# Undilated key-major scores with the queries in natural order, and an exponential that reads its PSUM columns by residue of four

## The chip, the cores and the metric

The kernel runs on one core of one Trainium2 chip. The metric is the device time of one execution in microseconds (us). Five engines work beside each other on their own instruction queues: TensorE (PE in the profile, its weight loads as PEld), VectorE (DVE), ScalarE (ACT), GpSimd (POOL) and SyncE (SP), which issues nearly all DMAs. Matrix products land in PSUM, everything else lives in SBUF or in DRAM.

## The reference, cut to what matters

One decoder layer is computed for a prompt of 2048 tokens and a group of 32 sample tokens: a normalised input projection, retention heads and attention heads beside each other, an output projection, a SwiGLU block and a final norm. The change lies in the attention of the prompt: 8 heads of 64 dimensions, each with three patterns of window and dilation, (128, 1), (512, 4) and (2048, 16).

```
def banded_window_attention(q, k, v, n_back):
    ...
    s = jnp.einsum('nbihd,nbjhd->nbhij', qb, kb, preferred_element_type=jnp.float32) * ATT_SCALE
    ...
    mask = (dist >= 0) & (dist <= n_back) & (kj[:, None, :] >= 0)
    s = jnp.where(mask[None, :, None], s, -jnp.inf)
    lse = jax.nn.logsumexp(s, axis=-1)
    p = jnp.exp(s - lse[..., None])
    o = jnp.einsum('nbhij,nbjhd->nbihd', p, vb.astype(jnp.float32))

def dilated_attention_prompt(q, k, v):
    for window, dil in DILATED_GROUPS:
        ...
    return combine_by_denominator(outs, lses)
```

In every pattern a query sees the 129 keys at distances 0, dil, 2 dil, ... The three outputs are added with the weights of their softmax denominators, which is one softmax with a common maximum and a common sum.

## The kernel before

The program runs in phases: an input phase (`phase_in`), `attention`, `mixing`, the output projection (`phase_out`) and the SwiGLU block (`phase_ff`). Next to each other in time they share the engines, and the instruction order on each engine is the order in which the Python code emits them.

`attention` works head by head, and inside a head over 20 groups of units. A unit is 128 keys and the queries that see them. Groups 0 to 3 have dilation 16 (four units of 128 queries each). Then come, four times, two groups of dilation 4 and two groups of dilation 1, each of two units of 256 queries; where a unit stands at the end of the sequence it has 128. So a head has 8 groups of dilation 1, and the last of them has 384 query columns in place of 512.

For each group three things are done on TensorE:

- `weights` (tile `aB`, key-major: keys on partitions, queries in columns). One product of an identity with a mask (L863, or L865 where the two units differ in width) fills the PSUM bank with 0 or -1e30. Each unit then adds two products to its columns: L878 (128 rows: the keys' high and low halves against the high half of the queries) and L879 (66 rows: the low half of the queries, and the negated maximum). ScalarE takes the exponential out of PSUM (`p`, L883) and rounds it (`ph`, L884), and GpSimd, in some groups VectorE, forms the remainder (`pl`, L885). The bank pool of `aB` has two buffers.
- `values` (tile `acc`, L928 to L930), three products for each 128 query columns, with `ph` and `pl` as the moving operand. It comes three groups later (`LAG = 3`).
- `row_max` of a later head (tile `aS`, L811 and L813, query-major), whose maxima VectorE takes (L817). It runs in 16 of a head's 20 groups, and not at all beside the last head.

In the values of a dilation-1 group the query columns have to stand by residue of four (`e r i` in the code: 128-blocks, residue, index), because one accumulator bank of 512 columns (`acc`, `o_` in `values`) serves both dilation 4 and dilation 1 and is laid out by residue. Before the change this order is made by the score products: for `step == 1` the moving operand, the queries in SBUF, is read with a step of four fp32 elements, and the mask has a second copy in the same order:

```
mk = maskr[:, 1 if groups[gi][0][0] == 1 else 0]
...
if step == 1:
    s = s.rearrange("p (e r i) -> p e r i", r=4, i=32)
    q1, q2 = (a[:, t0:t0 + n].rearrange("p (e i r) -> p e r i", r=4, i=32) for a in (q1, q2))
```

The two mask copies are written once, by two casts each on ScalarE (L1003, L1004); for the second copy L1003 reads SBUF with the same step of four. In dilation-4 and dilation-16 groups the queries are read with a step of 4 and 16 elements, since they are the tokens of one residue.

Of the kernel before, what the change touches and what calls it, by code (L numbers as in the profile page):

```python
# [8 lines left out]
F32R = mybir.dt.float32r  # L9
AF = mybir.ActivationFunctionType  # L10
# [90 lines left out]
def hybrid_step(ctx: ExitStack, tc: tile.TileContext, i: dict, o: dict):  # L101
    nc = tc.nc
    pe, act, dve, pool, sp = nc.tensor, nc.scalar, nc.vector, nc.gpsimd, nc.sync

    def f32(ap):
        return ap.bitcast(F32)
# [639 lines left out]
    def attention(after):  # L746
# [4 lines left out]
        ro = P("ao", 1)  # L751
# [1 line left out]
        jk = P("aj", 2)  # L753
        pS = P("apS", 3, PSUM)
        mask = ro.tile([128, 256], F32, name="mask")
        maskr = ro.tile([128, 2, 384], F32R, name="maskr")
        names = ("kst", "qhh", "qll", "k2")
        sets = [[ro.tile([128, T], F32R, name=f"{n}0") for n in names]]
        H = {}
# [1 line left out]
        def load_qk(h):  # L761
            d = H[h] = {}
            ks, qh, ql, k2 = sets[h % 3]
            r = slice(h * 64, h * 64 + 64)
            for a in range(2):
                dma(ks[64 * a:64 * a + 64], d_qk[1][a][r, :])
                dma(qh[64 * a:64 * a + 64], d_qk[0][0][r, :])
            dma(ql[0:64], d_qk[0][1][r, :])
            if h > 2:
                dma(ql[64:66], d_z)  # L770
            dma(k2[0:64], d_qk[1][0][r, :])
            d.update(ks=ks, qh=qh, ql=ql, k2=k2, m=mp.tile([128, 48], F32, tag="m", name="m"))
# [11 lines left out]
        def unit(dil, b, r=0):  # L784
            if dil == 16:
                return 16, r, False, False, r, 32 + r
            if dil == 1:
                return 1, 128 * b, b > 0, b < 15, b, b
            return 4, 512 * b + r, b > 0, b < 3, 4 * b + r, 16 + 4 * b + r

        groups = [[unit(16, 0, 4 * g + r) for r in range(4)] for g in range(4)]
# [63 lines left out]
        def weights(h, gi):  # L855
            d = H[h]
            ps = pB.tile([128, 512], F32, tag="b", name="aB")
            off = 0
            ns = [256 if u[3] else 128 for u in groups[gi]]
            mk = maskr[:, 1 if groups[gi][0][0] == 1 else 0]  # L860
            if len(set(ns)) == 1:
                m_ = mk[:, 0:ns[0]].rearrange("p (o n) -> p o n", o=1).to_broadcast([128, len(ns), ns[0]])
                pe.matmul(ps[:, 0:sum(ns)].rearrange("p (o n) -> p o n", o=len(ns)), identr, m_, start=True, stop=False)  # L863
            else:
                pe.matmul(ps[:, 0:384], identr, mk, start=True, stop=False)  # L865
            for x, (step, t0, _, nxt, kt, _) in enumerate(groups[gi]):
                n = ns[x]
                s = ps[:, off:off + n]
                off += n
                kc = slice(t0, t0 + 127 * step + 1, step)  # L870
                q1, q2 = d["qh"], d["ql"][0:66]
                if step == 1:

                    s = s.rearrange("p (e r i) -> p e r i", r=4, i=32)
                    q1, q2 = (a[:, t0:t0 + n].rearrange("p (e i r) -> p e r i", r=4, i=32) for a in (q1, q2))
                else:
                    q1, q2 = (a[:, t0:t0 + (n - 1) * step + 1:step] for a in (q1, q2))
                pe.matmul(s, d["ks"][:, kc], q1, start=False, stop=False)  # L878
                pe.matmul(s, d["k2"][0:66, kc], q2, start=False, stop=(x == len(ns) - 1))  # L879
            p = pp.tile([128, 512], F32, tag="p", name="p")  # L880
            hi = ptp.tile([128, 512], F32R, tag="ph", name="ph")
            lo = ptp.tile([128, 512], F32R, tag="pl", name="pl")
            act.activation(p[:, 0:off], ps[:, 0:off], AF.Exp)  # L883
            act.copy(hi[:, 0:off], p[:, 0:off])  # L884
            (dve if gi in DV[h] else pool).tensor_tensor(lo[:, 0:off], p[:, 0:off], f32(hi[:, 0:off]), ALU.subtract)  # L885
            return h, gi, hi, lo
# [94 lines left out]
        def ones(t):  # L981

            for x, v in ((3, 1.0), (2, 0.0)):
                dve.tensor_scalar(t[x][64:66], zero[64:66, 0:1].to_broadcast([2, T]), v, None, ALU.add)
# [12 lines left out]
        junk = jk.tile([128, 512], F32, tag="j", name="junk")[:, 0:256]  # L997
        dma(junk, i["k_maskt"])
        load_qk(0)
        for a in range(2):  # L1000
            v = junk if a == 0 else junk.rearrange("p (e i r) -> p e r i", r=4, i=32)
            w = maskr[:, a, 0:256]
            act.copy(w if a == 0 else w.rearrange("p (e r i) -> p e r i", r=4, i=32), v)  # L1003
            act.copy(maskr[:, a, 256:384], f32(maskr[:, a, 0:128]))  # L1004
        ones(sets[0])
        dma(d_z, sets[0][2][64:66])

# [56 lines left out]
        for n in range(last + 8):  # L1064
            tick()
            h, s = divmod(n, NG)
            if 0 <= h < NAH:
                q.append(weights(h, s))
                if s == 0 and h + 2 < NAH:
                    load_qk(h + 2)  # L1070
# [11 lines left out]
            if q and (len(q) > LAG or h == NAH):  # L1082
                a = q.pop(0)
# [1164 lines left out]
    with tc.manual_schedule():  # L2248
        R = {}
        tl = tail(R)  # L2250
        mix = mixing(tl, R)
        att = attention(mix)
        phase_in(att)
        for g in (att, mix, tl):
            for _ in g:
                pass
# [32 lines left out]
```

## Time and profile before

| what | value |
|---|---|
| device time, three runs | 3094.52, 3107.44, 3107.82 us, median 3107.44 us |
| the profiled execution, its own time | 3105.31 us |
| its span, first to last instruction | 3103.5 us |
| mean granted TensorE clock of the span | 0.961 |
| busy: PE, PEld | 2976.6 us (96%), 2631.2 us (85%) |
| busy: DVE, ACT, POOL | 1736.1 us (56%), 1118.3 us (36%), 1649.2 us (53%) |

The page counts busy time per engine; the spans of matrix products overlap in it, so the pace of TensorE is read from the distance between the starts of neighbouring products in the timeline. The score products of `weights` run from 721.6 to about 1188 us of the span. The granted clock is given as a share of 2.4 GHz: 1.00 is 2.4 GHz and 0.50 is 1.2 GHz.

### The profile page before, as it was taken

To read this page: it belongs to the slowest core of one execution; us is meant where nothing else is said; L and a number is where in the kernel's file an instruction comes from. 1 tells how busy PE (TensorE), PEld (TensorE's weight loads), DVE (VectorE), ACT (ScalarE), POOL (GpSimd) and SP (SyncE) were. 2 spreads that over 40 slices of the span, in tenths; PEclk is the share of its full clock that TensorE was granted. 3 is DMA by queue.
4 is the path that set the end of the run, shared out by engine and by line. 5 is a ranking of instruction groups with operands and counts; after the bars stand their busy time and mean duration, and the time that the engine had idled before them with its cause. 6 is when DMAs were issued, how large, how long until landed. Compare 5 with 4: busy or idle time off the path is not lost.

```text
span 3103.5 us, 47148 instructions
## 1 busy us (share of the span) xinstructions
PE 2976.6 (96%) x16898; PEld 2631.2 (85%) x16898; DVE 1736.1 (56%) x3234; ACT 1118.3 (36%) x2197; POOL 1649.2 (53%) x1316
## 2 busy tenths in 40 slices
PE   8999999999999997989996999999999999999998
PEld 4777888889999996777885899999999998888886
DVE  6424533023333434674665998767767673555766
ACT  5333422303444453464443444333333334111222
POOL 4546746401333332464555778666666666443774
PEclk9999999998879988999997999999999999999999
DMA  6454745735565426774696436533443334241432
GB/s 233 154 172 152 232 131 159 221 83 133 120 137 122 106 57 178 233 257 158 182 284 190 139 112 196 162 107 99 176 146 90 100 100 142 96 152 55 156 130 100
DMA packets 395237, 461.71 MB, mean 149 GB/s; under 512 B 51869, under 2 KB 306141, under 8 KB 391862
## 3 DMA queue, kind: packets, MB, share of 16 engines
q1 hardware_dynamic: 394072, 457.61, 48.6%
q8 instruction: 134, 2.20, 0.3%
q10 hardware_dynamic: 930, 1.07, 0.1%
q14 instruction: 101, 0.83, 0.1%
HBM read 335.79 MB, written 122.81 MB: 148 GB/s over the span
## 4 chain that ended last, share of the span: by engine, by line
PE 77%; POOL 6%; DVE 5%; issue 5%; DMA 3%; ACT 1%; SPq 0%; POOLq 0%; ACTq 0%; DVEq 0%
PE fg L2005 8%; PE fg L2003 8%; PE fg L2002 8%; PE fd L2142 5%; PE fd L2143 5%; PE fd L2141 5%; PE z L523 5%; PE z L524 5%; PE z L528 5%; PE aB L879 3%; PE aB L878 3%; POOL op L1921 3%; PE aS L811 2%; PE aS L813 2%; PE aB L863 2%
## 5 line engine op out<-in xcount | busy, mean ns | idle before, releaser
L2002 PE MATMUL fg<-B,op 128*128 128x256 f32 (+2 forms) x1848 | 579.8, 324 | 39.4 <-ACT op L1919 33.4
L2003 PE MATMUL fg<-B,op 128*128 128x256 f32 (+2 forms) x1848 | 578.1, 323 | 0.0
L1921 POOL TENSOR_TENSOR op<-s,op 128x512 fp32r<-128x512 f32 x253 | 381.5, 1526 | 156.2 <-ACT op L1919 107.2
L2002 PEld LDWEIGHTS fg<-B,op 128*128 128x128 f32 x1848 | 353.2, 191 | 43.1 <-ACT op L1919 37.0
L2005 PE MATMUL fg<-B,op 128*128 128x256 f32 (+2 forms) x1848 | 372.7, 324 | 1.9 <-POOL op L1921 1.6
L2003 PEld LDWEIGHTS fg<-B,op 128*128 128x128 f32 x1848 | 353.1, 191 | 0.5
L2084 POOL TENSOR_TENSOR op<-raw,op 128x512 fp32r<-128x512 f32 x174 | 231.5, 1355 | 201.4 <-ACT op L2083 197.0
L2148 DVE TENSOR_TENSOR acc<-fd,acc 128x512 f32<-128x512 f32 x330 | 223.7, 688 | 190.7 <-PE fd L2143 190.7
L885 POOL TENSOR_TENSOR pl<-p,ph 128x512 fp32r<-128x512 f32 (+2 forms) x128 | 155.3, 1213 | 313.3 <-ACT ph L884 235.6
L1921 POOL TENSOR_TENSOR op<-raw,op 128x512 fp32r<-128x512 f32 x176 | 249.2, 1430 | 126.3 <-ACT op L1919 126.3
L2005 PEld LDWEIGHTS fg<-B,op 128*128 128x128 f32 x1848 | 310.0, 191 | 4.4 <-POOL op L1921 4.2
L523 PE MATMUL z<-w,hh 128*128 128x512 f32 x768 | 310.9, 405 | 2.0 <-ACT w L318 1.7
L524 PE MATMUL z<-w,hh 128*128 128x512 f32 x768 | 305.5, 398 | 0.9 <-DVE w L319 0.9
L817 DVE CUSTOM_DVE_ANT_0 junk<-aS,mask 128x256 f32<-128x256 f32 (+1 forms) x384 | 121.0, 363 | 294.7 <-PE aS L813 293.4
L2142 PE MATMUL fd<-op,op 128*128 128x512 f32 x704 | 275.9, 392 | 2.8 <-POOL op L2084 2.5
L2141 PE MATMUL fd<-op,op 128*128 128x512 f32 x704 | 275.2, 391 | 0.0
L2143 PE MATMUL fd<-op,op 128*128 128x512 f32 x704 | 275.0, 391 | 0.0
L2024 ACT ACTIVATE sg<-sg 128x256 f32<-128x256 f32 (+2 forms) x132 | 65.2, 494 | 556.5 <-DVE sg L2019 556.5
L2083 ACT CAST op<-raw 128x512 fp32r<-128x512 f32 x176 | 98.8, 617 | 306.8 <-issue 153.1
L528 PE MATMUL z<-w,hl 128*128 128x512 f32 x768 | 192.2, 392 | 0.0
L523 PEld LDWEIGHTS z<-w,hh 128*128 128x128 f32 x768 | 147.2, 192 | 34.8 <-ACT w L318 2.1
L524 PEld LDWEIGHTS z<-w,hh 128*128 128x128 f32 x768 | 147.4, 192 | 31.8 <-DVE w L319 1.5
(363 smaller groups left out, 6875.2 us busy)
## 6 DMA issues: line engine op xcount, KB each, us to landing
raw<-in_w_gate SPq DMA_DIRECT2D x66, 512.0 KB
raw<-in_w_up SPq DMA_DIRECT2D x66, 512.0 KB
raw<-in_w_in SPq DMA_DIRECT2D x96, 256.0 KB
raw<-d_ff SPq DMA_DIRECT2D x44, 512.0 KB
raw<-in_w_down SPq DMA_DIRECT2D x44, 512.0 KB
d_B<-op SPq DMA_DIRECT2D x74, 256.0 KB
d_ff<-sg SPq DMA_DIRECT2D x88, 192.0 KB
ar<-in_w_ada SPq DMA_DIRECT2D x32, 512.0 KB
```

Of the source, the lines that this page charges most:

```text
L523: pe.matmul(ps, hh[:, k, :], hi[:, k, :], start=(k == 0), stop=False)
L524: pe.matmul(ps, hh[:, k, :], lo[:, k, :], start=False, stop=False)
L528: pe.matmul(ps, hl[:, k, :], hi[:, k, :], start=False, stop=(k == 7))
L1921: eng.tensor_tensor(lo, src, f32(hi), ALU.subtract)
L2002: pe.matmul(ps, hi[:, k], xh[:, k], start=(k == 0), stop=False)
L2003: pe.matmul(ps, hi[:, k], xl[:, k], start=False, stop=False)
L2005: pe.matmul(ps, lo[:, k], xh[:, k], start=False, stop=(k == 3))
L2084: (dve if q == 0 and idx in (3, 7) else pool).tensor_tensor(lo, src, f32(hi), ALU.subtract)
L2141: pe.matmul(ps, f[0][:, tt], d[0], start=(y == 0), stop=False)
L2142: pe.matmul(ps, f[0][:, tt], d[1], start=False, stop=False)
L2143: pe.matmul(ps, f[1][:, tt], d[0], start=False, stop=(y == len(todo) - 1))
L2148: dve.tensor_tensor(to, ps, to, ALU.add)
```

## The change

For dilation 1, `weights` reads the queries in natural order, as contiguous columns, and writes the scores to PSUM in natural order. The mask copy by residue goes, and with it two casts; all dilations use the one mask. The exponential (L883) now makes the order: for dilation-1 groups its input, the PSUM bank, is read with a step of four fp32 elements and its output `p` is written contiguously by residue. Dilations 4 and 16, `row_max`, the rounding, the remainder and the values are as before.

```
-        maskr = ro.tile([128, 2, 384], F32R, name="maskr")
+        maskr = ro.tile([128, 384], F32R, name="maskr")
...
-            mk = maskr[:, 1 if groups[gi][0][0] == 1 else 0]
+            mk = maskr
...
-                if step == 1:
-
-                    s = s.rearrange("p (e r i) -> p e r i", r=4, i=32)
-                    q1, q2 = (a[:, t0:t0 + n].rearrange("p (e i r) -> p e r i", r=4, i=32) for a in (q1, q2))
-                else:
-                    q1, q2 = (a[:, t0:t0 + (n - 1) * step + 1:step] for a in (q1, q2))
+                q1, q2 = (a[:, t0:t0 + (n - 1) * step + 1:step] for a in (q1, q2))
                 pe.matmul(s, d["ks"][:, kc], q1, start=False, stop=False)
                 pe.matmul(s, d["k2"][0:66, kc], q2, start=False, stop=(x == len(ns) - 1))
...
-            act.activation(p[:, 0:off], ps[:, 0:off], AF.Exp)
+            po, pi = p[:, 0:off], ps[:, 0:off]
+            if groups[gi][0][0] == 1:
+
+                po = po.rearrange("p (e r i) -> p e r i", r=4, i=32)
+                pi = pi.rearrange("p (e i r) -> p e r i", r=4, i=32)
+            act.activation(po, pi, AF.Exp)
...
-        for a in range(2):
-            v = junk if a == 0 else junk.rearrange("p (e i r) -> p e r i", r=4, i=32)
-            w = maskr[:, a, 0:256]
-            act.copy(w if a == 0 else w.rearrange("p (e r i) -> p e r i", r=4, i=32), v)
-            act.copy(maskr[:, a, 256:384], f32(maskr[:, a, 0:128]))
+        act.copy(maskr[:, 0:256], junk)
+        act.copy(maskr[:, 256:384], f32(maskr[:, 0:128]))
```

The order of the instructions is the same on PE, DVE, POOL and SP. On ACT it differs in one place, where the mask is prepared beside the input phase (`zav` and `vst` belong to the input projection, `maskr` to the mask):

```order
 L556 COPY zav<-z 128x512
 L560 CAST vst_250<-zav 128x8x64
-L1003 CAST maskr<-junk 128x256
-L1004 CAST maskr<-maskr 128x128
-L1003 CAST maskr<-junk 128x256
-L1004 CAST maskr<-maskr 128x128
+L1000 CAST maskr<-junk 128x256
+L1001 CAST maskr<-maskr 128x128
```

Two of the four casts are gone, and nothing else has moved.

## Rows read from the trace of the kernel before

**Rows 1.** The page: busy time (share, instructions), and the chain that ended last.
```profile
PE 2976.6 (96%) x16898; PEld 2631.2 (85%) x16898; DVE 1736.1 (56%) x3234; ACT 1118.3 (36%) x2197; POOL 1649.2 (53%) x1316
...
PE 77%; POOL 6%; DVE 5%; issue 5%; DMA 3%; ACT 1%; SPq 0%; POOLq 0%; ACTq 0%; DVEq 0%
```

**Rows 2.** Stretches: start:end, length, busy per engine (instructions), granted clock, DMA share, GB/s.
```profile
720.00:1189.00 469.00, 469.00 (x3335) 454.47 (x3333) 184.50 (x751) 220.12 (x354) 155.12 (x130) 0.87 0.49 113
...
940.00:946.00 6.00, 6.00 (x58) 5.66 (x57) 1.75 (x9) 3.30 (x6) 2.56 (x2) 1.00 0.30 68
770.70:777.50 6.80, 6.80 (x43) 6.70 (x42) 1.44 (x12) 0.91 (x3) 0.73 (x1) 0.50 0.00 0
```

**Rows 3.** Timeline, PE (start, length): a dilation-1 group of `weights`, clock 1.00.
```profile
943.64 0.44 PE L863 MATMUL aB<-maskr,identr 128*128 128x512 f32 x1
943.92 0.39 PE L878 MATMUL aB<-qhh,kst 128*128 128x256 f32 x1
944.13 0.41 PE L879 MATMUL aB<-qll,k 66*128 66x256 f32 x1
944.37 0.41 PE L878 MATMUL aB<-qhh,kst 128*128 128x256 f32 x1
944.60 0.41 PE L879 MATMUL aB<-qll,k 66*128 66x256 f32 x1
944.83 0.24 PE L928 MATMUL acc<-ph,v 128*66 128x128 f32 x1
```

**Rows 4.** Timeline, PE: dilation-1 products of `row_max`, contiguous keys moving, clock 1.00.
```profile
940.12 0.28 PE L811 MATMUL aS<-kst,qhh 128*128 128x256 f32 x1
940.24 0.29 PE L813 MATMUL aS<-k,qll 66*128 66x256 f32 x1
...
940.85 0.22 PE L928 MATMUL acc<-ph,v 128*66 128x128 f32 x1
```

**Rows 5.** Timeline, PE, clock 0.50: a dilation-1 group of `weights`, then contiguous `row_max`.
```profile
775.62 0.74 PE L863 MATMUL aB<-maskr,identr 128*128 128x512 f32 x1
776.16 0.42 PE L878 MATMUL aB<-qhh,kst 128*128 128x256 f32 x1
...
777.11 0.29 PE L811 MATMUL aS<-kst,qhh 128*128 128x128 f32 x1
...
800.20 0.41 PE L811 MATMUL aS<-kst,qhh 128*128 128x256 f32 x1
...
801.06 0.31 PE L928 MATMUL acc<-ph,v 128*66 128x128 f32 x1
```

**Rows 6.** Groups on ACT, 720 to 1189 us: count | busy us, mean ns | idle before.
```profile
L884 ACT CAST ph<-p 128x512 fp32r<-128x512 f32 x136 | 84.3, 620 | 4.4
L883 ACT ACTIVATE p<-aB 128x512 f32<-128x512 f32 x136 | 81.5, 599 | 175.5 <-PE aB L879 175.5
L933 ACT COPY y<-acc 66x512 f32<-66x512 f32 x32 | 34.4, 1076 | 15.1 <-PE acc L930 15.0
...
L883 ACT ACTIVATE p<-aB 128x384 f32<-128x384 f32 x8 | 3.9, 492 | 10.0 <-PE aB L879 10.0
```

**Rows 7.** Timeline, ACT: the two mask casts, contiguous read, then read in steps of four.
```profile
598.68 0.40 ACT L1003 CAST maskr<-junk 128x256 fp32r<-128x256 f32 x1
...
599.32 0.65 ACT L1003 CAST maskr<-junk 128x256 fp32r<-128x256 f32 x1
```

**Rows 8.** Timeline, ACT, last head, with the idle time before: pace without `row_max`.
```profile
1169.45 0.60 ACT L883 ACTIVATE p<-aB 128x512 f32<-128x512 f32 x1 [0.64 <-PE aB L879]
1170.08 0.62 ACT L884 CAST ph<-p 128x512 fp32r<-128x512 f32 x1
1171.46 0.60 ACT L883 ACTIVATE p<-aB 128x512 f32<-128x512 f32 x1 [0.76 <-PE aB L879]
```

**Rows 9.** Groups of all engines, 720 to 1189 us: GpSimd's remainder.
```profile
L885 POOL TENSOR_TENSOR pl<-p,ph 128x512 fp32r<-128x512 f32 (+1 forms) x127 | 154.3, 1215 | 310.2 <-ACT ph L884 232.6 <-PE aS L813 41.6 <-PE acc L930 12.3
```

**Rows 10.** Timeline, all engines: the end of `attention` and the first product of `mixing`.
```profile
1188.35 0.49 ACT L883 ACTIVATE p<-aB 128x384 f32<-128x384 f32 x1 [0.34 <-PE aB L879]
...
1189.29 0.61 ACT L1430 COPY qpad<-zero 128x512 f32<-128x512 f32 x1
...
1189.93 1.28 SPq L112 DMA_DIRECT2D qpad<-d_rT  x2
...
1193.76 2.04 PE L1153 MATMUL rsc<-qpad,rkT 128*128 128x128 f32 x8 [4.72 <-DMA rkT<-d_rT]
```

## The prediction

> **What bounds the kernel now.** I read the page first: TensorE is busy for 96% of the span, and the chain that ended last is 77% TensorE [rows 1]. Then the table of stretches for the part that the change touches, from the first score product at about 720 us to the last at 1189 us: TensorE is busy for 469.00 of 469.00 us, ScalarE for 220.12, GpSimd for 155.12, and the mean granted clock is 0.87 [rows 2]. So here the end is set by how fast TensorE gets through its own list, and by nothing that it waits for. Third, the timeline of single products, since busy time of overlapping products says nothing of their pace; the reader is to take differences of starts. A dilation-1 group of `weights` at full clock goes from 943.64 to 944.83, 1.19 us: the mask product holds the engine for 0.28 us, and the four score products for 0.21, 0.24, 0.23 and 0.23 us [rows 3]. Right beside them stand products of the same sizes (256 columns, 128 and 66 rows, contiguous weights) whose moving operand is contiguous: six starts from 940.12 to 940.85, 0.122 us each [rows 4]. The granted clock is 1.00 around both [rows 2]. The one thing in which the two differ is the step of four with which `weights` reads the queries. That step costs a factor of 1.9, and the change takes it away.
>
> **The change part by part.** There are 8 heads with 8 dilation-1 groups, 64 in all; 8 of them have 384 columns, as the count of the narrow exponentials says [rows 6].
>
> Score products at full clock. In the timeline 50 of the 56 wide groups start at clock 1.00, each 1.19 to 1.21 us long like the one shown [rows 3]. After the change I expect the mask's 0.28 us as before (its columns, its bank and its type stay) and 4 x 0.122 = 0.49 us, so 0.77 us, a saving of 0.42 us. 50 x 0.42 = 21.0 us. What is uncertain is the mask's step: 512 contiguous columns at the pace of the contiguous products would be 2 x 0.122 = 0.24 us, and if the 0.28 us includes something that the strided successor causes, it falls to that: saving 0.46 us, 23 us in all. On the other side, if accumulating on the mask costs each product 0.01 us more than in `row_max`, the saving is 0.38 us, 19 us in all. I take 0.42, because the mask product itself is untouched.
>
> Score products at half clock. The other 6 wide groups fall into stretches with clock 0.50 such as 770.7 to 777.5 [rows 2]. One takes from 775.62 to 777.11, 1.49 us, the mask 0.54 us of it and the strided products 0.24 us each as at full clock. Contiguous ones of this size take (801.06 - 800.20)/4 = 0.215 us at that clock [rows 5]. So strided reading hides the slow clock, and the gain there is small: 1.49 - (0.54 + 4 x 0.215) = 0.09 us, 6 x 0.09 = 0.5 us.
>
> The 8 narrow groups have three quarters of the columns: 6 at full clock at 0.75 x 0.42 = 0.32 us, and 2 that begin at half clock at about 0.1 us: 2.1 us.
>
> Together TensorE's list gets 21.0 + 0.5 + 2.1 = 23.6 us shorter.
>
> The exponential. It reads PSUM with a step of 16 bytes in place of a contiguous run. No row shows ScalarE reading PSUM with that step. The nearest are: the same step out of SBUF, where a cast of 256 columns went from 0.40 to 0.65 us, 0.98 ns per element more [rows 7]; and a copy that writes SBUF with a step of 64 bytes, 1.076 us for 512 columns where a contiguous PSUM read and write of that size is 0.599 us, 0.93 ns per element more [rows 6]. From below, the price is nothing: 0.60 us as before. I take the first row, since it has the same step: 0.60 + 512 x 0.98 ns = 1.10 us. On ScalarE that is 56 x 0.50 + 8 x 0.38 = 31 us more. The cover is ScalarE's idle time: 220 us busy in 469 us become 251 us in 445 us. The tightest place is the last head, where no `row_max` fills the gaps: there ScalarE is idle 0.64 to 0.76 us before each exponential, and groups follow at 1.9 to 2.0 us [rows 8]. With the change two dilation-1 groups follow each other at about 1.5 us and want 1.10 + 0.62 = 1.72 us of ScalarE each, then come two dilation-4 groups at 1.9 to 2.0 us that want 1.22 us. Over four groups that is 5.9 us of ScalarE in 6.9 us of TensorE. ScalarE falls behind by some 0.4 us inside the pair and catches up. Two things wait for it: the bank of `aB`, which is wanted again two groups later, and the values, which come three groups later. From the end of a group's scores to its values there are then over 4 us, and the chain of exponential, rounding and remainder takes 1.10 + 0.62 + 1.22 = 2.9 us plus handovers [rows 6, 9]. So I cost the slower exponential at nothing, but for one place.
>
> That place is the end. The last exponential is a narrow dilation-1 one; behind it in ScalarE's queue stands the copy of zeros to `qpad`, and behind that the first loads of `mixing`, for which TensorE waits 4.72 us [rows 10]. There ScalarE's chain sets the end: the last two exponentials take 0.50 and 0.38 us longer, against some 0.75 us that TensorE saves in the last two groups. I take 0.8 us off.
>
> The casts. Two fewer on ScalarE near 600 us, 0.65 us and a shorter one [rows 7]; they lie beside input products, so nothing. Instruction order elsewhere is unchanged, so no wait moves past another. DMAs: TensorE has no idle time in the stretch [rows 2], and the loads for the next head have most of a head's time; a head that is 3 us shorter out of 58.6 (469/8) leaves that as it is.
>
> Sum: 23.6 - 0.8 = 22.8 us. Against the profiled execution, 3105.3 - 22.8 = 3082.5 us. It lies 2.1 us under the median of the three runs, 3107.4, which would give 3084.6. I forecast **3083 us**.
>
> **A rule against it.** The trace shows 0.23 us against 0.122 us for strided and contiguous reading [rows 3, 4]. The Trainium skill ("SBUF — State Buffer", section "Door 1: The DMA port swizzle", its note on cachelines) says that an SBUF read may step over up to 4 fp32 elements for free. By that rule a step of exactly 4 would cost nothing and the sum would be zero; its own reason, lines of 16 bytes that want two hits each, rather agrees with the trace, since at this step each element has a line of its own.
>
> **The rivals.** *The clock comes up with it.* In the stretch the granted clock is 0.87, which is 0.26 of 469 us, some 122 us, at half clock [rows 2]; it falls where strided dilation-16 products stand close together, as around 770 us. Dilation-1 groups become denser, and some slow stretches may end earlier or not begin. A contiguous product loses 0.215 - 0.122 us there, about 43% of its time, a strided one next to nothing [rows 3 to 5]; with half of the slow time spent in contiguous products, all of it costs some 26 us. A third of that back: 3083 - 9 = 3074 us. For it: the work gets denser. Against: the causes, dilation 16 and dilation 4, stay strided.
>
> *The clock goes the other way.* With dilation-1 groups shorter, the strided dilation-16 products make up more of each stretch, and the share at half clock rises from 0.26 to 0.4: of 445 us some 60 us more, at 0.21 lost (half of 43%) 13 us. That gives 3096 us, within what counts as no change. For it: dense work gains nothing at half clock. Against: the clock stays at 1.00 in stretches where strided and contiguous work alternate, as at 940 to 946 us [rows 2].
>
> *The step is not the cause.* If the 0.23 us came from accumulating on the mask, or from the pace at which the bank is written, nothing would change and the time stays at 3107 us. For it: `row_max` has no mask before it, and it is the only comparison. Against: in half-clock stretches the strided products keep their 0.24 us while contiguous ones go from 0.122 to 0.215 us [rows 4, 5], so something that does not run at TensorE's clock limits them.
>
> *ScalarE becomes the bound; slower than before.* If a strided PSUM read were far dearer than the SBUF one, the exponentials would set the pace. Per head ScalarE otherwise needs 20 roundings, 12 other exponentials and 4 copies, about 20 x 0.62 + 12 x 0.60 + 4 x 1.08 = 24 us [rows 6]. Local stalls in the last head begin when an exponential takes over 1.6 us, since then four groups want more than 6.9 us. A loss against before begins when 8 exponentials fill the rest of 58.6 us, at 4.3 us each, seven times today's. At 5 us each a head takes 64 us, 8 x 5.4 = 43 us more: 3150 us. Against: both rows of a strided ScalarE operand stay under twice the price [rows 6, 7].
>
> **How the numbers follow.** The forecast with its bounds, 3077 to 3090 (19 to 23 us on the wide groups, runs that lie several us apart): 0.73. Clock better, 3074: 0.11. Clock worse or a local stall, 3096: 0.08. Step not the cause, 3107: 0.05. ScalarE bound, 3150: 0.03. The range runs from 3070, below the better clock, to 3096, where the worse one begins to be left out; that leaves less than 2 in 10 outside. A measurement of this kernel tells about 0.5% from no change, that is below 3092 or above 3123 us. Faster: 0.73 + 0.11, and a little of the third case, 0.85. Same: 0.12. Slower: 0.03.
>
> **What would show it.** Right: the starts of dilation-1 score products 0.12 us apart at full clock and a group of `weights` near 0.77 us; the exponentials of dilation 1 at 1.1 us, those of dilations 4 and 16 still at 0.60; TensorE busy all through, and the first product of `mixing` some 23 us earlier. Wrong: products still 0.23 us apart; TensorE idle ahead of L928 or L863 with ScalarE or GpSimd as the releaser; a mean granted clock in the stretch well away from 0.87; or the 23 us present at the end of `attention` and gone by the end of the span, because the loads of `mixing`, which begin when attention's buffers close, set the later pace.

## The result

| | kernel before | changed kernel |
|---|---|---|
| device time, median of 5 runs | 3105.57 us (3092.26 to 3107.82) | 3072.55 us (3066.88 to 3077.74) |
| the profiled execution: time, span | 3105.31, 3103.5 us | 3070.15, 3068.4 us |
| first and last score product of `weights` | 721.8, 1188.0 us | 714.6, 1152.5 us |
| first product of `mixing` | 1193.8 us | 1158.2 us |

The ratio of the times is 0.9908, with a 95% interval of 0.9887 to 0.9929. By the ratio the change makes the kernel 28.6 us faster (22 to 35 us); the two medians lie 33 us apart. The forecast was 3083 us, from a sum of 22.8 us; the time is 10 us below it and inside the range of 3070 to 3096.

The two profiled spans differ by 35 us, more than the ratio gives. The table tells where: 7.2 us lie ahead of the first score product, 28.3 us inside attention, and behind it nothing (from the first product of `mixing` to the end of the span 1909.7 us before and 1910.2 us after). Ahead of attention the change takes away only two small casts on ScalarE. Second traces put the first score product at 713.2 us in the kernel before and at 714.9 us in the changed one, so the 7 us are a difference between executions.

The page of the changed kernel, beside [rows 1]: busy time (share, instructions), and the chain that ended last.

```profile
PE 2946.1 (96%) x16898; PEld 2612.7 (85%) x16898; DVE 1732.0 (56%) x3234; ACT 1115.2 (36%) x2195; POOL 1649.1 (54%) x1316
...
PE 76%; POOL 6%; issue 5%; DVE 4%; DMA 4%; ACT 1%; SPq 1%; POOLq 0%; ACTq 0%; DVEq 0%
```

Attention as a stretch, beside [rows 2] (start:end, length, busy per engine with instructions, granted clock, DMA share, GB/s), in the changed kernel:

```profile
714.60:1152.50 437.90, 437.48 (x3312) 429.87 (x3310) 182.62 (x749) 216.36 (x351) 154.35 (x128) 0.88 0.53 121
```

TensorE still sets the pace: it is busy for 437.48 of 437.90 us (the other 0.4 us are one wait for a load in the last head), and ScalarE's busy time is where it was, at 216 us, not 31 us higher.

Two dilation-1 groups in a row, timeline of PE, beside [rows 3]:

```profile
921.75 0.45 PE L863 MATMUL aB<-maskr,identr 128*128 128x512 f32 x1
922.04 0.28 PE L873 MATMUL aB<-qhh,kst 128*128 128x256 f32 x1
922.15 0.28 PE L874 MATMUL aB<-qll,k 66*128 66x256 f32 x1
922.27 0.29 PE L873 MATMUL aB<-qhh,kst 128*128 128x256 f32 x1
922.39 0.29 PE L874 MATMUL aB<-qll,k 66*128 66x256 f32 x1
922.52 0.22 PE L928 MATMUL acc<-ph,v 128*66 128x128 f32 x1
...
923.25 0.44 PE L863 MATMUL aB<-maskr,identr 128*128 128x512 f32 x1
```

The mask product holds the engine for 0.29 us, the four score products for 0.11 to 0.13 us each: 0.77 us a group in place of 1.19, and the next group follows after 1.50 us in place of 1.94.

The exponentials, groups on ACT by shape (count | busy us, mean ns | idle before), beside [rows 6]:

```profile
L883 ACT ACTIVATE p<-aB 128x512 f32<-128x512 f32 x136 | 81.8, 602 | 152.1 <-PE aB L874 150.8 <-DVE pl L885 1.3
...
L883 ACT ACTIVATE p<-aB 128x384 f32<-128x384 f32 x8 | 3.9, 491 | 8.0 <-PE aB L874 7.9
```

602 ns against 599 before, though 56 of the 136 now read PSUM in steps of 16 bytes, and 491 against 492 ns for the eight narrow ones, all of which do. The step costs ScalarE nothing.

Summing the distances between starts in both timelines by kind of work, attention splits so:

| us | before | changed |
|---|---|---|
| mask and scores, dilation 1 (64 groups) | 76.4 | 52.0 |
| mask and scores, dilation 4 | 76.9 | 76.6 |
| mask and scores, dilation 16 | 63.6 | 62.9 |
| `row_max` | 123.0 | 123.0 |
| values | 126.2 | 123.2 |
| all of it | 466.3 | 437.9 |
| of this at half clock | 122.5 | 102.4 |

24.4 us are the dilation-1 products themselves. The other 4 us are work that the change does not touch, 3 us of them the values, which spend less time at half clock.

### The profile page after: what moved, and what is told of

It reads as the page before. It is cut to its first block, busy times and chain, and to the rows that moved or that the text cites. A ratio compares the mean times of both kernels' runs of the same rounds, so it can differ in the third digit from the quotient of the medians.

```text
span 3068.4 us, 47145 instructions
## 1 busy us (share of the span) xinstructions
PE 2946.1 (96%) x16898; PEld 2612.7 (85%) x16898; DVE 1732.0 (56%) x3234; ACT 1115.2 (36%) x2195; POOL 1649.1 (54%) x1316
## 4 chain that ended last, share of the span: by engine, by line
PE 76%; POOL 6%; issue 5%; DVE 4%; DMA 4%; ACT 1%; SPq 1%; POOLq 0%; ACTq 0%; DVEq 0%
PE fg L2002 8%; PE fg L2000 8%; PE fg L1999 8%; PE z L523 5%; PE z L524 5%; PE z L528 5%; PE fd L2139 5%; PE fd L2140 5%; PE fd L2138 5%; POOL op L1918 3%; PE aS L811 3%; PE aS L813 2%; PE aB L874 2%; PE aB L873 2%; PE aB L863 2%
```

## The experiments

What follows asks three things: whether the 24.4 us are the query step and nothing else; why ScalarE did not feel the stepped read, and how much it could have borne; and what the other 4 us and more are. Second traces come first, since every comparison of traces rests on how far two executions of one kernel lie apart.

**The two kernels once more.** No edit. These executions took 3097.20 us (kernel before) and 3063.38 us (changed kernel).

> The kernel before once more, for a second trace: in the first one the first score product came at 721.8 us and 122.5 us of attention's 466 us stood at half clock; a kernel whose dilation-1 products were the same had 109 us. Theory A (half clock in attention varies by tens of us between executions of one kernel, as 102 and 71 us did in two executions of the changed one): between 75 and 130 us. Theory B (sparser dilation-1 groups keep it high): 105 to 125 us again. Attention's length follows at about 0.2 us for each us at half clock: 456 to 466 us under A, 462 to 466 us under B.

> The changed kernel once more, for a second trace: how much of attention stands at half clock, and how long the input phase takes, in another execution. In the first trace 102 us of attention's 438 us were at half clock, and the first score product came at 714.6 us (721.8 us in the kernel before). Theory A (the time at half clock is a matter of where a head falls against the clock's own grid, and varies from execution to execution): it differs by 10 us or more from the first trace. Theory B (denser dilation-1 groups hold the clock up): within a few us of 102 us.

The stretch of attention in the second trace of the kernel before, and in that of the changed kernel:

```profile
713.20:1176.30 463.10, 463.10 (x3311) 449.26 (x3310) 182.40 (x749) 219.05 (x351) 154.74 (x128) 0.88 0.49 114
```

```profile
714.90:1145.90 431.00, 430.75 (x3311) 423.56 (x3310) 182.52 (x749) 215.79 (x351) 154.39 (x128) 0.92 0.54 123
```

The kernel before stood at half clock for 109 us of attention (122.5 in the first trace), the changed one for 71 us (102). The dilation-1 groups sum to 76.6 and 52.1 us, as in the first traces. So the products repeat to 0.2 us, and attention as a whole to 3 and 7 us, with the time at half clock going the same way. For the kernel before, 109 us is what both theories allowed; for the changed kernel, 71 us against 102 us speaks for variation between executions.

**The exponential in natural order.** The changed kernel with `act.activation(p[:, 0:off], ps[:, 0:off], AF.Exp)` for every dilation.

> The changed kernel with the exponential of dilation 1 reading PSUM contiguously; the reordering by residue is left out, so the dilation-1 probabilities meet the wrong values. Theory (a PSUM read in steps of 16 bytes costs ScalarE nothing): exponentials of 512 columns 0.60 us in all groups, as in the changed kernel, and its time, 3066 to 3078 us. Rival (the stepped read costs something that TensorE feels although the exponential's own duration does not show it): faster than the changed kernel by 5 us or more.

Measured: 3071.25 us, ratio to the kernel before 0.9916 (0.9891 to 0.9941), the changed kernel's 0.9908 inside it. Exponentials of 512 columns take 603 ns on average and those of 384 columns 492 ns. The 56 wide ones of dilation 1 by themselves take 609 ns here, reading contiguously, and 608 ns in the changed kernel, reading in steps. The stepped PSUM read costs neither ScalarE nor TensorE anything that shows.

**The reordering on the output side.** The same reordering, done by where the exponential writes:

```
-                po = po.rearrange("p (e r i) -> p e r i", r=4, i=32)
-                pi = pi.rearrange("p (e i r) -> p e r i", r=4, i=32)
+                po = po.rearrange("p (e r i) -> p e i r", r=4, i=32)
+                pi = pi.rearrange("p (e i r) -> p e i r", r=4, i=32)
```

> The changed kernel with the reordering on the exponential's output side: PSUM is read contiguously and SBUF is written in steps of 128 bytes. Theory 1 (a stepped SBUF write costs ScalarE some 0.93 ns per element, as the copy of 66x512 in the kernel before): exponentials of dilation 1 at about 1.08 us, those of dilation 4 and 16 at 0.60 us. Theory 2, the prediction's cover (ScalarE's idle time takes up an exponential of 1.1 us, except 0.8 us at the end of attention): the time of the changed kernel within 3 us, TensorE without waits for ScalarE or GpSimd inside attention. Rival (two dear exponentials in a row delay the bank or the values): 5 to 15 us slower than the changed kernel, with TensorE idle ahead of the mask or values products in the last head.

The groups on ACT by shape, and the stretch of attention:

```profile
L883 ACT ACTIVATE p<-aB 128x512 f32<-128x512 f32 x136 | 110.4, 812 | 127.8 <-PE aB L874 124.6 <-DVE pl L885 1.5 <-POOL pl L885 1.1
L883 ACT ACTIVATE p<-aB 128x384 f32<-128x384 f32 x8 | 7.1, 882 | 4.9 <-PE aB L874 4.9
```

```profile
720.30:1151.40 431.10, 430.34 (x3311) 423.01 (x3310) 183.61 (x749) 244.59 (x350) 154.24 (x128) 0.91 0.53 123
```

With 0.599 us for the 80 groups of the other dilations, the 56 of dilation 1 take (110.4 - 80 x 0.599)/56 = 1.12 us each. That is the price the prediction had put on the stepped read, 1.10 us, paid here for a stepped write to SBUF. And the time is 3069.55 us, ratio 0.9907 (0.9889 to 0.9924), the same as the changed kernel's. ScalarE is 28 us busier and TensorE does not feel it inside attention: its waits for an exponential sum to 0.5 us. So the cover in the prediction holds at 1.1 us, though the change itself never needed it.

The prediction's one exception, the end of attention, can be seen here too. The copy to `qpad`, the first load of `rkT` and the first product of `mixing`, in the changed kernel and in this run:

```profile
1153.75 0.61 ACT L1427 COPY qpad<-zero 128x512 f32<-128x512 f32 x1
1155.77 0.54 SPq L112 DMA_DIRECT2D rkT<-d_rT  x1
1158.19 1.19 PE L1150 MATMUL rsc<-qpad,rkT 128*128 128x128 f32 x4 [4.69 <-DMA rkT<-d_rT]
```

```profile
1153.36 0.61 ACT L1427 COPY qpad<-zero 128x512 f32<-128x512 f32 x1
1155.38 0.54 SPq L112 DMA_DIRECT2D rkT<-d_rT  x1
1159.24 0.98 PE L1150 MATMUL rsc<-qpad,rkT 128*128 128x128 f32 x3 [6.84 <-DMA rkT<-d_rT]
```

Counted from the last score product (1152.5 and 1151.4 us), the load is issued 0.7 us later here, close to the 0.8 us of the sum, and the product comes 2.1 us later. The rest of the 2.1 us need not be the exponential's: in two runs with exponentials of 0.60 us (stepped and short, and other operands, below) the load is issued at the usual time and the product comes 1.2 us late all the same.

**The stepped exponential without the contiguous queries.** The kernel before, with the changed kernel's exponential.

> The kernel before, with the stepped query read kept and the exponential reading PSUM in steps as well (the columns are reordered twice, so the dilation-1 probabilities meet the wrong values). It has one half of the change, the stepped exponential, without the other. Theory (the gain is the query read alone): dilation-1 score products 0.23 us apart, exponentials 0.60 us, time that of the kernel before, 3092 to 3108 us, ratio to it 0.998 to 1.002. Rival (part of the gain comes from elsewhere, for instance from the mask or from the exponential): faster than the kernel before by 4 us or more.

Score products of a dilation-1 group, timeline of PE:

```profile
939.42 0.39 PE L878 MATMUL aB<-qhh,kst 128*128 128x256 f32 x1
939.63 0.41 PE L879 MATMUL aB<-qll,k 66*128 66x256 f32 x1
939.86 0.41 PE L878 MATMUL aB<-qhh,kst 128*128 128x256 f32 x1
```

Measured: 3099.78 us, ratio 0.9999 (0.9987 to 1.0011). The exponentials are at 599 ns, the dilation-1 products 0.226 us apart on average at full clock and their groups, with the mask, sum to 76.5 us. Taking back the contiguous query read, with the mask copy that goes with it, loses the whole gain, and the mask's product takes 0.284 us in both kernels.

**One step per head.** In the changed kernel, the dilation-1 queries are read as

```
+                    rr_ = (1, 2, 4, 8, 16, 32, 2)[h]
+                    q1, q2 = (a[:, t0:t0 + n].rearrange("p (i r) -> p r i", r=rr_) for a in (q1, q2))
...
+                    q1, q2 = (a[:, t0:t0 + n].rearrange("p (i q r) -> p q i r", q=2, r=2) for a in (q1, q2))
```

in heads 0 to 6 and in head 7.

> The changed kernel with the dilation-1 queries read in another pattern in each head (columns then stand in the wrong order): heads 0 to 6 with a step of 1, 2, 4, 8, 16, 32 and 2 elements of 4 bytes, head 7 in pairs of neighbours with a step of 4 elements between pairs. It measures the price of the step on a product of 256 columns at full clock. Theory A (each element that lies in another 16-byte line than the one before costs an access of its own): step 1 0.12 us, step 2 between 0.12 and 0.18 us, step 4 0.235 us, pairs about 0.12 to 0.18 us. For steps 8 and 16 the kernel before shows 0.217 us for 128 columns at step 16, so 0.43 us for 256, and step 8 between 0.235 and 0.43 us. Theory B (any step other than 1 costs the same factor): 0.235 us for every step above 1, 0.12 us at step 1.

Timeline, PE, two neighbouring products each: head 0 (step 1), head 1 (step 2), head 5 (step 32), head 7 (pairs):

```profile
743.75 0.28 PE L882 MATMUL aB<-qll,k 66*128 66x256 f32 x1
743.87 0.28 PE L881 MATMUL aB<-qhh,kst 128*128 128x256 f32 x1
...
803.29 0.41 PE L882 MATMUL aB<-qll,k 66*128 66x256 f32 x1
803.52 0.41 PE L881 MATMUL aB<-qhh,kst 128*128 128x256 f32 x1
...
1056.01 0.40 PE L882 MATMUL aB<-qll,k 66*128 66x256 f32 x1
1056.23 0.40 PE L881 MATMUL aB<-qhh,kst 128*128 128x256 f32 x1
...
1160.15 0.41 PE L882 MATMUL aB<-qll,k 66*128 66x256 f32 x1
1160.38 0.41 PE L881 MATMUL aB<-qhh,kst 128*128 128x256 f32 x1
```

The medians over a head at full clock are 0.120 us for step 1 and 0.230, 0.232, 0.217, 0.218 and 0.221 us for steps 2, 4, 8, 16 and 32; pairs cost 0.227 us. (The kernel ran in 3092.6 us, one execution.) Theory A falls at both ends: pairs share a 16-byte line and gain nothing, and step 16 costs no more than step 4. Every order tried but the contiguous one moves the columns at about half pace, 256 columns in 0.22 to 0.23 us. And since all these products follow the same mask product into the same kind of bank, it is the order of reading, and nothing about the mask or the bank, that makes the difference. The Trainium skill's note on cachelines ("SBUF — State Buffer", section "Door 1: The DMA port swizzle"), by which up to 4 fp32 elements may be stepped over for free, does not hold for this operand of TensorE: the measurement decides, and it says a factor of 1.8 to 1.9 from step 2 on.

**Which operand is stepped.** That left the 0.217 us of a dilation-16 product, which has only 128 columns. In the changed kernel's dilations 4 and 16:

```
+                if step > 1 and h in (0, 1, 4, 5):
+                    q1, q2 = (a[:, 0:n] for a in (q1, q2))
...
+                if step > 1 and h in (2, 3, 4, 5):
+                    kc = slice(0, 128)
```

> The changed kernel with other operands in the key-major scores of dilations 4 and 16 (data of other tokens): heads 0 and 1 read the queries (moving) contiguously and load the keys (weights) in steps, heads 2 and 3 the other way round, heads 4 and 5 both contiguously, heads 6 and 7 as before. Dilation-16 products (128 columns) are 0.217 us apart and dilation-4 ones (256 columns) 0.235 us. Theory A (the price per product is the larger of a moving read at half pace and a weight load at half or less): stepped weights alone leave 128 columns at about 0.21 us and give 256 columns some 0.21 us; stepped queries alone give 128 columns 0.11 us and leave 256 columns at 0.235 us; both contiguous give 0.06 and 0.12 us. Theory B (the moving read alone sets the pace): stepped weights alone give 0.06 and 0.12 us.

Timeline: dilation 4 in head 1 (stepped weights, contiguous queries) and in head 5 (both contiguous), then dilation 16 in head 3 (stepped queries, contiguous weights) and in head 5 (both contiguous):

```profile
807.51 0.39 PE L879 MATMUL aB<-qll,k 66*128 66x256 f32 x1
807.61 0.33 PEld L878 LDWEIGHTS aB<-qhh,kst 128*128 128x128 f32 x1
807.74 0.40 PE L878 MATMUL aB<-qhh,kst 128*128 128x256 f32 x1
...
1023.53 0.29 PE L879 MATMUL aB<-qll,k 66*128 66x256 f32 x1
1023.53 0.19 PEld L878 LDWEIGHTS aB<-qhh,kst 128*128 128x128 f32 x1
1023.65 0.28 PE L878 MATMUL aB<-qhh,kst 128*128 128x256 f32 x1
```

```profile
898.52 0.29 PE L878 MATMUL aB<-qhh,kst 128*128 128x128 f32 x1
898.63 0.29 PE L879 MATMUL aB<-qll,k 66*128 66x128 f32 x1
...
1008.48 0.27 PE L879 MATMUL aB<-qll,k 66*128 66x128 f32 x1
1008.59 0.28 PE L878 MATMUL aB<-qhh,kst 128*128 128x128 f32 x1
```

Stepped weights alone keep a product at 0.23 us with 256 columns and at 0.218 us (median) with 128; stepped queries alone cost 0.11 us with 128 columns and 0.232 us (median) with 256. So theory A holds in its main line: each operand has its price and the larger one counts, some 0.22 us for stepped weights of 128 columns, 0.11 us per 128 columns for a stepped moving operand. One number missed: both contiguous, 128 columns take 0.11 us, not 0.06. A load of 128 contiguous weight columns seems to set that floor (the values products, 128 moving columns with 64 or 66 weight columns, follow each other at 0.06 us); it is not told apart here. The kernel ran in 3061 us (one execution). That does not tell what contiguous operands would be worth: the second trace of the changed kernel had 3063 us, TensorE waited 7.3 us for VectorE's maxima in heads 2 to 5, which it does not do in the changed kernel, and the data were other tokens'.

**The mask product at the end.** The changed kernel with L863 moved behind the score products of its group, the first of which opens the bank.

> The changed kernel with the mask product at the end of each group in place of the start. In both kernels the mask product holds TensorE for 0.285 us at full clock, where 512 contiguous columns elsewhere take about 0.23 us. Theory A (the 0.055 us more belongs to the product that opens the bank, or to the loading of the keys behind it): it goes or shrinks, up to 160 x 0.055 = 9 us faster than the changed kernel. Theory B (it belongs to the mask product wherever it stands): the time of the changed kernel within 3 us, and the values that follow start 0.28 us after it.

Measured: 3081.69 us, ratio 0.9930 (0.9909 to 0.9951), some 9 us behind the changed kernel by the medians. Timeline, PE, a dilation-16 group:

```profile
902.83 0.41 PE L868 MATMUL aB<-qhh,kst 128*128 128x128 f32 x1
903.07 0.39 PE L869 MATMUL aB<-qll,k 66*128 66x128 f32 x1
...
904.58 0.43 PE L872 MATMUL aB<-maskr,identr 128*128 128x512 f32 x1
904.85 0.28 PE L811 MATMUL aS<-kst,qhh 128*128 128x256 f32 x1
```

The mask product still holds the engine for 0.27 us here (0.24 us before the values of a dilation-1 group), and dilation-1 groups take 0.770 us at full clock against 0.762 us: there is no gain, and the kernel is slower than either theory had it. In a dilation-1 group 0.05 us only change place: the mask takes 0.234 us in place of 0.284 (medians), and the score product that now opens the group 0.170 us in place of 0.117. But a dilation-16 group takes 2.07 us in place of 1.92, a dilation-4 group 1.29 in place of 1.18. With the mask first, the two opening products of a dilation-16 group take 0.29 + 0.10 us (medians), the second far under its usual 0.217 us; with the mask last, they are 0.24 and 0.217 us. In a dilation-4 group the opening score product takes 0.365 us in place of 0.215. It looks as if a contiguous product ahead of stepped ones took part of the first one's price; why is not shown. What is shown is that the mask's 0.285 us is not waste that could be had back by moving it.

**The exponential made longer.** In the changed kernel, `for _ in range(3 if groups[gi][0][0] == 1 else 1)` around the exponential, then with 8.

> The changed kernel with each dilation-1 exponential issued three times over the same data, some 1.75 us of ScalarE in place of 0.60. The prediction put local stalls in the last head beyond 1.6 us, and a loss against the kernel before only beyond 4.3 us. Its cover: ScalarE goes from 212 us busy in 430 to about 285, and the time stays within 6 us of the changed kernel, with TensorE's waits in the last head alone. Rival (the three-group lag or the two banks give way earlier): TensorE waits in every head, 10 to 25 us slower than the changed kernel.

> The changed kernel with each dilation-1 exponential issued eight times, some 4.3 us of ScalarE, about where the prediction put the loss against the kernel before. By the prediction's count (ScalarE against TensorE over a whole head) a head's ScalarE work, 8 x 4.9 + 12 x 1.2 + 4.3 = 58 us, passes TensorE's 54 us by little: attention some 460 to 475 us, time 3095 to 3110 us. Rival (the pair of dilation-1 groups stalls TensorE within the head, since two banks and a lag of three groups even out only a few us): attention beyond 500 us, time over 3130 us.

Waits of TensorE (us in total, times, longest) with three and with eight exponentials, and attention as a stretch with eight:

```profile
PE aB L863 <- ACT p L884: 5.4, 13, 1.1
```

```profile
PE aB L863 <- ACT p L884: 104.7, 44, 3.7
```

```profile
720.00:1325.00 605.00, 500.16 (x3271) 481.73 (x3271) 178.72 (x740) 461.56 (x780) 154.29 (x126) 0.70 0.37 87
```

With three: 3085.49 us, ratio 0.9947 (0.9931 to 0.9963), 13 us behind the changed kernel, and waits in every head: 0.2 us in each of heads 1 to 5, 1.5 us in head 0, 0.6 us in head 6 and 2.2 us in the last. The waits give 5.4 of the 13 us; the first product of `mixing` comes 2 us later behind the last score product; the rest is not located. With eight: 3258 us (one execution). Both times the rival named in the expectation holds. The wait is for the bank: the mask product of a group needs the exponential of the group two before it. Two dilation-1 groups follow each other, so eight exponentials come twice as 5.0 us, with one rounding between them, in one block on ScalarE, and TensorE has only the next groups' work to put beside it:

```profile
929.24 5.00 ACT L884 ACTIVATE p<-aB 128x512 f32<-128x512 f32 x8 [3.16 <-PE aB L874]
934.27 0.62 ACT L885 CAST ph<-p 128x512 fp32r<-128x512 f32 x1
934.80 4.99 ACT L884 ACTIVATE p<-aB 128x512 f32<-128x512 f32 x8
```

With eight, TensorE also runs at half clock for far longer: a granted clock of 0.70 over 605 us is some 360 us at half clock, against 102 us in the changed kernel. So of the 174 us by which attention is longer, 105 us are waits, and most of the rest is slower products.

**Density or length.** To see where the clock's share comes from: the changed kernel with its dilation-1 score products issued twice (`for y in range(2 if step == 1 else 1)` around both), contiguous and long; and the kernel before without the 66-row products of dilation 1, stepped and short. They ran in 3126.7 and 3071.9 us, one execution each.

> The changed kernel with the four dilation-1 score products of each group issued twice (the scores of dilation 1 are doubled): contiguous as in the changed kernel, but a group takes about 1.24 us, as long as in the kernel before. Theory A (density holds the clock up): at most 100 us of attention at half clock, in an attention of about 462 us. Theory B (the length of a head against the clock's own grid decides): half clock as in the kernel before, 109 to 123 us, attention about 466 us.

> The kernel before with the 66-row products of dilation 1 left out: the queries are still read in steps, and a group takes about 0.73 us, as short as in the changed kernel's 0.76. Theory A (density): 105 us or more of attention at half clock. Theory B (length): 70 to 102 us, as in the executions of the changed kernel. Either way the dilation-1 groups sum to about 48 to 52 us in place of 76 us.

Attention in the one and in the other:

```profile
723.50:1207.90 484.40, 484.40 (x3567) 476.05 (x3566) 181.38 (x750) 218.58 (x351) 154.02 (x128) 0.83 0.47 109
```

```profile
721.90:1153.90 432.00, 431.54 (x3183) 420.24 (x3182) 182.73 (x749) 216.08 (x351) 154.58 (x128) 0.89 0.53 122
```

| time of attention at half clock | long dilation-1 groups | short ones |
|---|---|---|
| stepped queries | 122.5, 109 (kernel before), 109 (both steps) | 95 |
| contiguous queries | 160 | 102, 71 (changed kernel), 75, 75 (exponential contiguous, stepped write) |

The dense long kernel stands at half clock for longer than any other in the table, 160 us, which speaks against density holding the clock up. Its groups also came out longer than expected, 87 us in all, 19 us of it at half clock. The short ones all lie under the long ones, which speaks for length. But the two new corners have one execution each, the changed kernel alone spreads over 31 us, and the twice issued products lengthen a head by more than the change shortened it. What decides the length of these stretches is not settled by these runs.

Where the clock falls can be read from the traces, though. In the four traces of the two kernels it falls in two places of a head, and in no other. One is the end of heads 0 to 5, every time, for 6.8 or 10.2 us, while TensorE is in a row of twelve `row_max` products (dilations 16 and 4, 128 stepped columns each, 0.22 us apart) or just behind it. The other is among the dilation-16 scores at the start of some heads, for 3 to 17 us. In the changed kernel's first trace, head 0's end and head 1's start:

```profile
760.65:767.35 6.70, 6.70 (x42) 6.60 (x42) 1.91 (x16) 0.79 (x2) 0.73 (x1) 0.50 0.00 0
774.25:791.25 17.00, 17.00 (x94) 16.61 (x93) 5.06 (x22) 5.92 (x9) 4.98 (x5) 0.50 1.06 229
```

The ends sum to 51 and 55 us in the kernel before and to 58 and 55 us in the changed one; the starts to 72 and 55 us before and to 44 and 17 us after. So the shorter time at half clock lies at the heads' starts, in work that the change leaves as it was; why it is shorter there is not shown.

## Why the prediction was right, and where it was off

**What bounds the kernel** was right: TensorE's own list, with no waits in attention before and one of 0.4 us after.

**Score products.** 23.6 us were expected, 24.4 measured; the group at 0.77 us is as worked out, the mask's step unchanged at 0.285 us. The comparison with `row_max` carried it: stepped against contiguous, columns, rows and weights equal. The run with both steps shows that the stepped exponential gives nothing without the query read, the run with a contiguous exponential that it costs nothing, and the run with one step per head that the step alone makes a product slow.

**The exponential** was mis-sized: 1.10 us was taken from the row of the same step out of SBUF [rows 7], and the stepped read of PSUM takes 0.60 us, the lower bound. The nearer row was the wrong one, since it had the step right and the memory wrong. It cost little, because the term lay under cover; only the 0.8 us at the end of attention hung on it, and from the last score product to the first of `mixing` there are 5.7 us as before. With exponentials that do take 1.12 us (the stepped write) the load that `mixing` waits for is issued 0.7 us later, so that term was right for the price it was worked out from.

**The clock** is the rest. Between the first traces attention lost 28.3 us and the dilation-1 groups 24.4; the other 3.9 us are values at half clock (3.0 us) and small differences in dilations 4 and 16. Between the second traces it is 32.1 and 24.5 us. Rival 1 (the clock comes up with it, 9 us) had the right direction, with 3.9 and 7.6 us of its 9, but its reason, denser work, is not borne out by the dense long kernel. Its remark on where the clock falls was right in the main: where stepped products of 128 columns stand close together, in `row_max` and in the dilation-16 scores. The forecast's 22.8 us lie inside the measured 22 to 35 us; what the 28.6 us have beyond the products' 24.4 is the clock, two executions of one kernel differ by as much, and the cause stays open.

**The step is not the cause** fell with the run of one step per head: behind the same mask product, 0.120 us at step 1 and 0.230 us at step 2. **ScalarE becomes the bound** did not happen, but the price that the prediction set on a slower exponential was too low: it averaged ScalarE's work over a head and put a loss against the kernel before at 4.3 us per exponential and local stalls, in the last head alone, at 1.6 us. Three exponentials, some 1.8 us, already stalled TensorE in every head and cost 13 us. For 5 us each the prediction had 64 us a head and 3150 us; eight exponentials took 5.0 us and gave 78.5 us a head (heads 1 to 5), an attention of 611 us and 3258 us, with ScalarE still idle for a quarter of it. The step that failed in this rival is the averaging, and the half clock that came with the waits was not in it: with two banks, what counts is ScalarE's work on two groups in a row against TensorE's work in the same time.

## What to carry to other kernels

Where TensorE is busy all the time, look at the start-to-start distance of its products, and compare two that differ in one operand's order; a moving operand that is not contiguous went at about half pace here at full clock, whatever its step, and stepped weights of 128 columns cost 0.22 us a product. If an order is needed, put it where it is free: reading PSUM in steps of 16 bytes with ScalarE cost nothing, reading or writing SBUF in steps about 1 ns per element. And count cover over as many groups as there are buffers, not over a whole phase.

## What the runs showed of the hardware that was not expected

- ScalarE read 512 PSUM columns in steps of 16 bytes in 608 ns, as contiguous ones in the same groups (609 ns); the same order made by a stepped write to SBUF took 1.12 us.
- TensorE's moving operand cost the same at steps of 2 to 32 fp32 elements and in pairs of neighbours, 0.217 to 0.232 us for 256 columns against 0.120 us, at full clock.
- In the four traces of the two kernels the clock fell to 0.50 inside attention in two places only: at twelve stepped `row_max` products in a row at the end of heads 0 to 5, and among the dilation-16 scores at the start of some heads.
- Two executions of one kernel stood at half clock for 102 and 71 us of the same attention, which moved it by 7 us.
